# FFN input products: third unit's P5 and P4 ahead of the first P3, last unit's P7 ahead of P2, first weight sum on VectorE

## The chip, the cores and the metric

The kernel runs on one core of a Trainium2 chip. The metric is the device time of one execution in microseconds (us), lower is better. Three runs of the kernel before gave 786.75, 789.37 and 789.67 us (median 789.37). One further execution was profiled.

## The reference, cut to what matters

One layer of a hybrid decoder block on 512 tokens of width 1024, in float32: three parallel token mixers, a merge and an output projection, then a gated feed-forward network (FFN). The change is in the input product of the FFN:

```python
h2 = rms_norm(x, g_pre_ffn) * (1 + scale2) + shift2
gt, up = jnp.split(h2 @ w_ffn_in, 2, axis=-1)     # 1024 -> 2 x 2816
f = (jax.nn.silu(gt) * up) @ w_ffn_out            # 2816 -> 1024
x = x + (gate2 * rms_norm(f, g_post_ffn)).astype(x.dtype)
```

## The kernel before

**Three passes per product.** Every weight piece w is split into `hi` (a cast on ScalarE, line 155, to the fp32r type in which TensorE multiplies) and `lo = w - hi` (VectorE, lines 157 and 159). Activations are split alike (`hbh`, `hbl`; `tx`). A product takes three matmuls: hi x hi, hi x lo, lo x hi. TensorE therefore needs, for its first three matmuls, the cast, and for the third the subtraction as well.

**Seven products in place of eight.** The hidden width 2816 is cut into 11 units of 2 x 128 channels. Tokens are cut in two halves of 256. A unit's 2 x 2 block product is done by a Winograd scheme with seven products P1 to P7 (`step`, line 1203; each 24 matmuls of 256 columns: 2 halves of gate and up x 4 slices x 3 passes). P6 is added onto a copy of P1. P2 is accumulated onto P1's PSUM bank, **P3 onto P5's PSUM bank**. Before P3 may write that bank, VectorE has to have read P5 alone: `gated_m1` (lines 1244, 1245 and 1247) forms c2 from P7, P6 (in `u2`), P5 and P4, and its second instruction, line 1245, is the one that reads P5.

**Weights.** A unit has four weight blocks. P1, P2, P4 and P7 use one block each (P7 after `wsum3`, line 306, has added another to it). P5, P6 and P3 use a running sum `s`: `wsum` makes s, GpSimd then adds further blocks to it by accumulating DMAs (line 319) between these products. For the first unit, s is not made by VectorE: SyncE loads one block a second time straight into s (line 299), an accumulating DMA adds the other (line 301), and a further one does this unit's `wsum3` (line 302).

**What sets the order.** Around here the program is written out by hand, engine by engine (`manual_schedule`): each engine works off its instructions in the order in which the Python code issues them. The table `WINO` says in which order weight pieces are split. `step(u, q, o, start, stop, ahead)` first has pieces split up to `ahead` beyond the one that it uses, and then issues its 24 matmuls. There are four buffers for `hi` and four for `lo`, so a cast four pieces ahead waits until TensorE has done with the product that used the buffer before. Instructions that wait hold up all that stands behind them on the same engine. The first three units are interleaved with the making of the activations (lines 1335 to 1417; `tar`, `b22` and `t3r` are sums and differences of the four blocks of h2, `hbh[:, 2]` and `hbh[:, 3]` the operands of P3 and P5); units 3 to 10 run in a loop (from line 1419). DMAs are queued on SyncE (loads) and GpSimd (accumulating ones).

Of the kernel before, what the change touches and what calls it, by code (L numbers as in the profile page):

```python
# [32 lines left out]
def hybrid_block(ctx: ExitStack, tc, x, c, mod_w, mod_b, g_pre_mix, g_post_mix, g_pre_ffn,  # L33
# [120 lines left out]
    def split(hi, lo, src, defer=False):  # L154
        act.copy(hi, src)  # L155
        if defer:
            lows_.append(lambda: vec.tensor_tensor(lo, src, hi.bitcast(F32), ALU.subtract))  # L157
        else:
            vec.tensor_tensor(lo, src, hi.bitcast(F32), ALU.subtract)  # L159
# [92 lines left out]

    WINO = [(0, 1), (1, 1), (0, 2), (2, 1), (1, 2), (2, 2)]
    WINO += [(u, q) for q in (5, 7, 6, 4) for u in range(2)]
    WINO += [(0, 3), (2, 5), (1, 3), (2, 4), (3, 5), (2, 6), (3, 1), (2, 7), (3, 4), (2, 3)]
    WINO += [(3, q) for q in (6, 2, 7)]
    for u in range(4, NU):
        WINO += [(u, 5), (u - 1, 3)] + [(u, q) for q in (1, 4, 6, 2, 7)]
    WINO.append((NU - 1, 3))
    units = {u: {} for u in range(NU)}  # L260
    late_pool = {}
# [1 line left out]
    def wino_src(u, i, g):  # L263
        c0 = g * FFN + (2 * u + i) * P
        return w_ffn_in[:, c0:c0 + P].rearrange("(k p) n -> p k n", k=8)
# [19 lines left out]
        units[u][i] = [raw[:, :, 4 * a:4 * a + 4].rearrange("p g k n -> p g (k n)")  # L285
                       for a in range(2)]

    def wsum_tile():
        return late_pool["fx"].tile([P, 2, 512], F32, tag="wsum", name="wsum", bufs=2)

    def wsum(u):

        un = units[u]
        un["s"] = wsum_tile()
        if u:
            vec.tensor_tensor(un["s"], un[1][0], un[1][1], ALU.add)  # L296
            return
        for g in range(2):
            nc.sync.dma_start(un["s"][:, g].rearrange("p (k n) -> p k n", k=4),
                              wino_src(u, 1, g)[:, 0:4])  # L300
        nc.gpsimd.dma_start(un["s"], un[1][1], accum_op=ALU.add)
        nc.gpsimd.dma_start(un[1][0], un[0][0], accum_op=ALU.add)

    def wsum3(u):
        un = units[u]
# [829 lines left out]
    def chain_h2(tb):  # L1135
        for hf in range(2):
            vec.scalar_tensor_tensor(xms[tb][hf], xms[tb][hf], sts[tb][:, 5:6], SH[hf],
                                     op0=ALU.mult, op1=ALU.add)
# [112 lines left out]
    def third_of(u, p5, u2):  # L1251

        step(u, 3, p5, False, True)
        vec.tensor_tensor(u2, p5, u2, ALU.add)
        gated_m0(f4s[u], u2, 1)
# [20 lines left out]
    if True:  # L1276
        def begin(n):

            while at["split"] < wino0 + n:
                split_piece(True)  # L1280
        late_mm(2)
        chain_sq(2, pos[2])
        chain_norm(2, pos[2])
        late_mm(3)
        begin(2)
        chain_x1(2, pos[2], lambda: t2("sq2"))
        lows()
        chain_xm(2)
        chain_sq(3, pos[3])
        chain_norm2(2)  # L1290
        chain_norm(3, pos[3])
        ma.close()
        fp = ctx.enter_context(tc.tile_pool(name="fp", bufs=1, reuse_waits="tile"))
        fxs = ExitStack()
        fx = fxs.enter_context(tc.tile_pool(name="fx", bufs=1, reuse_waits="tile"))
        late_pool.update(fp=fp, fx=fx)
        pb_ = {1: [], 5: [], 6: [], 7: [], 4: []}

        def fresh(q, ahead=0):
            u = len(pb_[q])  # L1300
            pb_[q].append(bank(f"pf{q}"))
            step(u, q, pb_[q][-1], True, True, ahead)
        u2s = [temp("u2", 512, 2) for _ in range(2)] + [f4_tile("u2f")[:, 0, :]]

        def first(u):
            fresh(1)
            act.copy(u2s[u], pb_[1][u])

        def sixth(ahead=0):
            u = len(pb_[6])  # L1310
            fresh(6, ahead)
            vec.tensor_tensor(u2s[u], pb_[6][u], u2s[u], ALU.add)


        ta, b22, t3_ = (f4_tile(n) for n in ("tar", "b22", "t3r"))

        def k4(t_, u):
            return t_[:, u, :].rearrange("p (k t) -> p k t", k=4)

        def tx_tiles(q):  # L1320
            tx[q] = [[q2("tx", FR).rearrange("p (k t) -> p k t", k=2) for _ in range(2)]
                     for _ in range(2)]

        def parts_of(q, t_):
            t4 = t_.rearrange("p u (k t) -> p k u t", k=4)
            for k0 in (0, 2):
                split(*[t__[k0 // 2].rearrange("p k (u t) -> p k u t", u=2) for t__ in tx[q]],
                      t4[:, k0:k0 + 2], True)
        tks = [slice(u * P, (u + 1) * P) for u in range(2)]

        def t1_of(u):
            vec.tensor_tensor(k4(ta, u), raws2[0, u], pts[u][0], ALU.subtract)
            split(hbh[:, 3, :, tks[u]], hbl[:, 3, :, tks[u]], k4(ta, u), True)
            act.copy(k4(b22, u), pts[u][1])
            lows()
        for u in range(3):
            wino_load(u, 1)
            if u == 0:
                wsum(u)
        begin(3)  # L1340
        first(0)
        lows()
        begin(4)
        first(1)
        chain_x1(3, pos[3], lambda: temp("sg1", 512))
        chain_h2(2)
        step(0, 2, pb_[1][0], False, True, 0)
        pts[0] = h2_tr(2)
        lows()
        begin(5)  # L1350
        chain_norm2(3)
        chain_xm(3)
        lows()
        chain_h2(3)
        first(2)
        begin(6)
        t1_of(0)
        step(1, 2, pb_[1][1], False, True, 0)
        pts[1] = h2_tr(3)
        begin(7)  # L1360
        t1_of(1)
        step(2, 2, pb_[1][2], False, True, 0)
        wsum(1)
        begin(8)
        act.preload_act_table_set("silu_and_others")
        for u in range(2):
            vec.tensor_tensor(k4(t3_, u), k4(b22, u), pts[u][0], ALU.subtract)
        lows()
        fresh(5)
        tx_tiles(7)  # L1370
        parts_of(7, t3_)
        lows()
        begin(9)
        lows()
        f4s.append(f4_tile("f4"))
        gated_m0(f4s[0], pb_[1][0], 0)
        flush()
        wsum3(1)
        fresh(5)
        f4s.append(f4_tile("f4"))  # L1380
        gated_m0(f4s[1], pb_[1][1], 0)
        tx_tiles(6)
        begin(10)
        vec.scalar_tensor_tensor(ta, ta, -1.0, b22, op0=ALU.mult, op1=ALU.subtract)
        lows()
        parts_of(6, ta)
        lows()
        fresh(7)
        begin(11)
        lows()  # L1390
        f4s.append(f4_tile("f4"))
        fresh(7)
        gated_m0(f4s[2], pb_[1][2], 0)
        begin(12)
        for q in range(2):
            vec.tensor_tensor(k4(ta, q), raws2[1, q], k4(ta, q), ALU.add)
        lows()
        tx_tiles(4)
        sixth()
        parts_of(4, ta)  # L1400
        lows()
        begin(13)
        lows()
        for u in range(2):
            split(hbh[:, 2, :, tks[u]], hbl[:, 2, :, tks[u]], k4(b22, u))
        sixth(3)
        for u in range(2):
            fresh(4, 4)
            flush()
            gated_m1(f4s[u], pb_[4][u], pb_[5][u], pb_[7][u], u2s[u])  # L1410
        third_of(0, pb_[5][0], u2s[0])
        fresh(5, 4)
        third_of(1, pb_[5][1], u2s[1])
        fresh(4, 4)

        third = None
        for u in range(3, NU):
            f4s.append(f4_tile("f4"))
            last = u == NU - 1
            p5 = bank("pf5")  # L1420
            step(u, 5, p5, True, True)
            if u == 3:
                sixth(4)
            else:
                third()
            if last:
                t_ = fp.tile([P, 2, 2, T], FR, tag="raw4", name="fparts", bufs=1)
                f_parts(0, t_[:, 0], t_[:, 1])
            p1 = bank("pf1")
            step(u, 1, p1, True, True)  # L1430
            if u == 3:
                fresh(7, 4)
                gated_m1(f4s[2], pb_[4][2], pb_[5][2], pb_[7][2], u2s[2])
            p6 = bank("pf6")
            act.copy(p6, p1)
            p4 = bank("pf4")
            step(u, 4, p4, True, True)
            if u == 3:
                third_of(2, pb_[5][2], u2s[2])
            step(u, 6, p6, False, True)  # L1440
            u2 = temp("u2", 512, 2)
            act.copy(u2, p6)
            step(u, 2, p1, False, True)
            gated_m0(f4s[u], p1, 0)
            p7 = bank("pf7")
            step(u, 7, p7, True, True)
            gated_m1(f4s[u], p4, p5, p7, u2)
            third = lambda a_=(u, p5, u2): third_of(*a_)
        f_split(1)
        third()  # L1450
        flush()
# [98 lines left out]
```

## Time and profile before

| | |
|---|---|
| runs, us | 786.75, 789.37, 789.67 |
| profiled execution, us | 787.89 |
| its span (first to last instruction), us | 786.0 |
| TensorE busy | 751.2 us, 96% |
| VectorE busy | 543.4 us, 69% |
| ScalarE busy | 398.0 us, 51% |
| FFN input products | 423.96 to 655.45 us of the span |
| of these, TensorE waiting | 5.4 (line 1245) + 1.2 + 1.0 + 0.3 us |

The times are microseconds from the first instruction. PE is TensorE, DVE is VectorE, ACT is ScalarE, POOL is GpSimd, SP is SyncE. A row of the timeline gives the start, the duration, the engine, the line, the operation, output<-inputs and, in square brackets, how long the engine stood idle before it and what released it. Matmuls overlap: each of these lasts 0.28 us, while one starts every 0.118 us.

### The profile page before, as it was taken

The page shows a single profiled execution, that of the slowest core. Times are in us where ns is not written, and L with a number is a line of the kernel's source. Part 1 is how long each engine was busy: PE and PEld are TensorE (multiplying, and loading weights), DVE is VectorE, ACT ScalarE, POOL GpSimd, SP SyncE. Part 2 cuts the span into 40 slices and gives each one's busy share as a digit, 9 for nine tenths or more (in the row PEclk, how much of TensorE's full clock was granted, in tenths as well). Part 3 has the DMA queues.
Part 4 walks back from the last instruction along what each step waited for, and adds up shares of the span by engine and source line. Part 5 has one row for each costly group of instructions (what it writes and reads, how often), then busy time and mean ns, then how long its engine had stood idle before and what let it go on. Part 6 is the DMA issues. An engine that isn't in the chain of part 4 may idle for free. (4 is left out here: it accounts for less than half of the span.)

```text
span 786.0 us, 11271 instructions
## 1 busy us (share of the span) xinstructions
PE 751.2 (96%) x4357; PEld 649.7 (83%) x4357; DVE 543.4 (69%) x769; ACT 398.0 (51%) x648; POOL 147.5 (19%) x191
## 2 busy tenths in 40 slices
PE   3899999999999999999999989999999999999996
PEld 2679887777678888888888889999999997878885
DVE  5999968668848656455688898777777778653114
ACT  5566544665668356353477554444444454523112
POOL 4453422244521110202100211111111100000000
PEclk9999999999999999999999999999999999999998
DMA  9982341112424686865848977767667654553002
GB/s 282 296 245 91 108 156 59 54 54 67 149 88 147 216 209 226 232 222 120 285 146 224 182 146 158 179 146 160 154 148 162 153 143 164 203 185 110 28 1 107
DMA packets 121061, 121.94 MB, mean 155 GB/s; under 512 B 4076, under 2 KB 94240, under 8 KB 121008
## 3 DMA queue, kind: packets, MB, share of 16 engines
q1 hardware_dynamic: 110128, 100.15, 41.5%
q0 software_dynamic: 10112, 20.01, 13.6%
q10 hardware_dynamic: 768, 1.07, 0.4%
q8 instruction: 34, 0.56, 0.3%
q14 instruction: 19, 0.16, 0.1%
HBM read 102.86 MB, written 2.10 MB: 134 GB/s over the span
## 5 line engine op out<-in xcount | busy, mean ns | idle before, releaser
L155 ACT CAST whi<-wraw 128x1024 fp32r<-128x1024 f32 (+1 forms) x129 | 133.0, 1035 | 160.9 <-PE pgt L168 32.6
L159 DVE TENSOR_TENSOR wlo<-wraw,whi 128x1024 fp32r<-128x1024 f32 (+1 forms) x89 | 110.0, 1242 | 82.9 <-ACT whi L155 82.3
L1221 PE MATMUL pf<-hbh,whi 128*128 128x256 f32 x352 | 99.5, 283 | 5.7 <-DVE c L1245 5.4
L1221 PE MATMUL pf<-hbl,whi 128*128 128x256 f32 x352 | 99.1, 282 | 1.0 <-DVE hbl L157 1.0
L1221 PE MATMUL pf<-hbh,wlo 128*128 128x256 f32 x352 | 99.2, 282 | 0.3 <-DVE wlo L157 0.3
L1221 PE MATMUL pf<-tx,whi 128*128 128x256 f32 x528 | 94.9, 281 | 0.0
L1221 PEld LDWEIGHTS pf<-tx,whi 128*128 128x128 f32 x528 | 80.9, 188 | 0.0
L167 PE MATMUL pgt<-hh,whi 128*128 128x512 f32 x192 | 75.6, 394 | 0.0
L1221 PE MATMUL pf<-tx,wlo 128*128 128x256 f32 x264 | 74.5, 282 | 1.0 <-DVE wlo L157 0.9
L169 PE MATMUL pgt<-hh,wlo 128*128 128x512 f32 x192 | 75.2, 392 | 0.0
L168 PE MATMUL pgt<-hl,whi 128*128 128x512 f32 x192 | 75.0, 391 | 0.0
L1221 PEld LDWEIGHTS pf<-hbh,whi 128*128 128x128 f32 x352 | 66.9, 190 | 6.3 <-issue 3.9
L1221 PEld LDWEIGHTS pf<-hbl,whi 128*128 128x128 f32 x352 | 66.7, 189 | 1.2 <-DVE hbl L157 1.2
L1221 PEld LDWEIGHTS pf<-hbh,wlo 128*128 128x128 f32 x352 | 66.8, 190 | 0.5 <-DVE wlo L157 0.5
L169 PE MATMUL pfo<-whi,fparts 128*128 128x512 f32 x154 | 60.9, 395 | 0.0
L168 PE MATMUL pfo<-wlo,fparts 128*128 128x512 f32 x154 | 60.9, 395 | 0.0
L167 PE MATMUL pfo<-whi,fparts 128*128 128x512 f32 x154 | 60.8, 395 | 0.0
L319 POOL DMA_DIRECT2D wsum<-wraw x22 | 26.2, 1191 | 176.7 <-DVE wlo L157 176.7
L157 DVE TENSOR_TENSOR wlo<-wsum,whi 128x1024 fp32r<-128x1024 f32 x33 | 40.4, 1225 | 25.7 <-ACT whi L155 25.6
L157 DVE TENSOR_TENSOR wlo<-wraw,whi 128x1024 fp32r<-128x1024 f32 x40 | 48.8, 1221 | 12.8 <-ACT whi L155 12.8
L155 ACT CAST whi<-wsum 128x1024 fp32r<-128x1024 f32 x33 | 34.4, 1047 | 42.5 <-DVE wsum L296 18.7
L1221 PEld LDWEIGHTS pf<-tx,wlo 128*128 128x128 f32 x264 | 49.7, 188 | 1.6 <-DVE wlo L157 1.6
(394 smaller groups left out, 1687.1 us busy)
## 6 DMA issues: line engine op xcount, KB each, us to landing
wraw<-in_w_in_dram SPq DMA_DIRECT2D x20, 1024.0 KB, 5.2
wraw<-in_w_ffn_in_dram SPq DMA_DIRECT2D x40, 512.0 KB, 5.8
wraw<-in_mod_w_dram SPq DMA_DIRECT2D x16, 1024.0 KB, 6.2
wsum<-wraw POOLq DMA_DIRECT2D x23, 512.0 KB, 5.5
wraw<-in_w_ffn_out_dram SPq DMA_DIRECT2D x10, 1024.0 KB, 5.1
wraw<-in_mod_w_dram SPq DMA_DIRECT2D x16, 512.0 KB, 6.3
wraw<-in_w_o_dram SPq DMA_DIRECT2D x8, 1024.0 KB, 5.7
gate<-gate POOLq DMA_DIRECT2D x14, 256.0 KB, 4.0
```

The source lines that it names most:

```text
L155: act.copy(hi, src)
L157: lows_.append(lambda: vec.tensor_tensor(lo, src, hi.bitcast(F32), ALU.subtract))
L159: vec.tensor_tensor(lo, src, hi.bitcast(F32), ALU.subtract)
L167: pe.matmul(o, whi, xhi, start=start, stop=False)
L168: pe.matmul(o, whi, xlo, start=False, stop=False)
L169: pe.matmul(o, wlo, xhi, start=False, stop=stop)
L319: lows_.append(lambda: nc.gpsimd.dma_start(un["s"], un[0][q - 5], accum_op=ALU.add))
L1221: pe.matmul(o[:, cs], a_[:, g, k, :], b_, start=(start and g + k + part == 0), stop=(stop and k == 3 and part == 2), skip_group_check=True)
```

## The change

It has three parts. (1) The products of the third unit (u = 2): its P5 and P4 now come right after the P4 of units 0 and 1, ahead of the P3 of units 0 and 1. In `WINO` the pieces move likewise, and the order of (2, 6) and (3, 5) is exchanged, as are the steps P6 of unit 2 and P5 of unit 3. The two P4 steps of units 0 and 1 look 3 pieces ahead instead of 4. The splitting of `hbh[:, 2]`, the operand of P3, is issued after the first `gated_m1` instead of ahead of it. The sum s of unit 2 gets a buffer of its own in another pool. (2) In the last unit (u = 10) P7 is issued ahead of P2, so that P2 stands between P7 and P3. (3) The sum s of unit 0 is made by VectorE from the two weight blocks in SBUF, behind `chain_h2(3)`; the two loads into s and one accumulating DMA go, and the other accumulating DMA (this unit's `wsum3`) is issued behind the sum.

```diff
-    WINO += [(0, 3), (2, 5), (1, 3), (2, 4), (3, 5), (2, 6), (3, 1), (2, 7), (3, 4), (2, 3)]
+    WINO += [(2, 5), (2, 4), (0, 3), (1, 3), (2, 6), (3, 5), (3, 1), (2, 7), (3, 4), (2, 3)]
...
+        WINO += [(u, q) for q in ((2, 7) if u < NU - 1 else (7, 2))]
...
     def wsum(u):
         un = units[u]
-        un["s"] = wsum_tile()
-        if u:
-            vec.tensor_tensor(un["s"], un[1][0], un[1][1], ALU.add)
-            return
-        for g in range(2):
-            nc.sync.dma_start(un["s"][:, g].rearrange("p (k n) -> p k n", k=4),
-                              wino_src(u, 1, g)[:, 0:4])
-        nc.gpsimd.dma_start(un["s"], un[1][1], accum_op=ALU.add)
-        nc.gpsimd.dma_start(un[1][0], un[0][0], accum_op=ALU.add)
+        if u == 2:
+            un["s"] = late_pool["fp"].tile([P, 2, T], F32, tag="f4", name="wsum2", bufs=NU)
+        else:
+            un["s"] = late_pool["fx"].tile([P, 2, 512], F32, tag="wsum", name="wsum", bufs=2)
+        vec.tensor_tensor(un["s"], un[1][0], un[1][1], ALU.add)
...
         chain_h2(3)
+        wsum(0)
+        nc.gpsimd.dma_start(units[0][1][0], units[0][0][0], accum_op=ALU.add)
         first(2)
...
-        for u in range(2):
-            split(hbh[:, 2, :, tks[u]], hbl[:, 2, :, tks[u]], k4(b22, u))
+        for i in (1, 0):
+            wino_load(3, i)
         sixth(3)
         for u in range(2):
-            fresh(4, 4)
+            fresh(4, 3)
             flush()
             gated_m1(f4s[u], pb_[4][u], pb_[5][u], pb_[7][u], u2s[u])
+            if u == 0:
+                for tb in range(2):
+                    split(hbh[:, 2, :, tks[tb]], hbl[:, 2, :, tks[tb]], k4(b22, tb))
+        fresh(5, 4)
+        fresh(4, 4)
         third_of(0, pb_[5][0], u2s[0])
-        fresh(5, 4)
         third_of(1, pb_[5][1], u2s[1])
-        fresh(4, 4)
...
-            step(u, 2, p1, False, True)
-            gated_m0(f4s[u], p1, 0)
             p7 = bank("pf7")
-            step(u, 7, p7, True, True)
-            gated_m1(f4s[u], p4, p5, p7, u2)
+            for q in (7, 2) if last else (2, 7):
+                if q == 2:
+                    step(u, 2, p1, False, True)
+                    gated_m0(f4s[u], p1, 0)
+                else:
+                    step(u, 7, p7, True, True)
+                    gated_m1(f4s[u], p4, p5, p7, u2)
```

In the program before, this is TensorE's order at the end of unit 1's P4 (`pf4_4295`): P3 of unit 0 follows, which writes the bank `pf5_4033` of that unit's P5.

```order
L1221 MATMUL pf4_4295<-tx_4183,whi_4225 128x256
L1221 MATMUL pf4_4295<-tx_4181,wlo_4226 128x256
L1221 MATMUL pf5_4033<-hbh_3359,whi_4256 128x256
L1221 MATMUL pf5_4033<-hbl_3360,whi_4256 128x256
L1221 MATMUL pf5_4033<-hbh_3359,wlo_4257 128x256
```

In the changed program it is P5 of unit 2 that follows, in a bank of its own, `pf5_4331`; P4 of unit 2 comes next, and only then P3 of unit 0.

```order
L1215 MATMUL pf4_4295<-tx_4181,whi_4225 128x256
L1215 MATMUL pf4_4295<-tx_4179,wlo_4226 128x256
L1215 MATMUL pf5_4331<-hbh_3359,whi_4258 128x256
L1215 MATMUL pf5_4331<-hbl_3360,whi_4258 128x256
L1215 MATMUL pf5_4331<-hbh_3359,wlo_4259 128x256
```

VectorE at the same place before; `wlo_4257` belongs to P3 of unit 0, `wlo_4263` to P5 of unit 2, the three `c2_4291` are unit 0's `gated_m1`, the three `c2_4327` unit 1's.

```order
L157 TENSOR_TENSOR wlo_4217<-wraw_3784,whi_4216 128x1024
L159 TENSOR_TENSOR hbl_3360<-b22_3782,hbh_3359 128x4x128 x2
L157 TENSOR_TENSOR wlo_4226<-rawf_3795,whi_4225 128x1024
L1230 TENSOR_TENSOR f4_4146<-sg0_4185,pf1_3922 128x256
L1312 TENSOR_TENSOR u2_3779<-pf6_4224,u2_3779 128x512
L157 TENSOR_TENSOR wlo_4257<-wsum_3787,whi_4256 128x1024
L296 TENSOR_TENSOR wsum_4260<-rawf_3798,rawf_3801 128x1024
L157 TENSOR_TENSOR wlo_4263<-wsum_4260,whi_4262 128x1024
L1244 TENSOR_TENSOR c2_4291<-pf7_4114,u2_3778 128x512
L1245 SCALAR_TENSOR_TENSOR c2_4291<-pf5_4033,c2_4291 128x512
L1247 TENSOR_TENSOR c2_4291<-pf4_4255,c2_4291 128x512
L157 TENSOR_TENSOR wlo_4297<-wsum_4023,whi_4296 128x1024
```

VectorE there in the changed program; `wlo_4259` belongs to P5 of unit 2, `wlo_4297` to P4 of unit 2, and `wlo_4333` of P3 of unit 0 follows behind the second three c2 instructions.

```order
L157 TENSOR_TENSOR wlo_4215<-wraw_3784,whi_4214 128x1024
L157 TENSOR_TENSOR wlo_4226<-rawf_3790,whi_4225 128x1024
L296 TENSOR_TENSOR wsum2_4229<-rawf_3793,rawf_3796 128x1024
L1224 TENSOR_TENSOR f4_4144<-sg0_4183,pf1_3920 128x256
L1306 TENSOR_TENSOR u2_3779<-pf6_4224,u2_3779 128x512
L157 TENSOR_TENSOR wlo_4259<-wsum2_4229,whi_4258 128x1024
L1238 TENSOR_TENSOR c2_4287<-pf7_4112,u2_3778 128x512
L1239 SCALAR_TENSOR_TENSOR c2_4287<-pf5_4031,c2_4287 128x512
L1241 TENSOR_TENSOR c2_4287<-pf4_4257,c2_4287 128x512
L159 TENSOR_TENSOR hbl_3360<-b22_3782,hbh_3359 128x4x128 x2
L157 TENSOR_TENSOR wlo_4297<-rawf_3796,whi_4296 128x1024
L1224 TENSOR_TENSOR f4_4068<-sg1_4300,c2_4287 128x512
```

The subtraction for one further piece no longer stands ahead of unit 0's three c2 instructions, and the two `hbl` splits moved from ahead of them to behind them.

VectorE where unit 0's sum is made, in the changed program; the row with `wsum_3917` is new there, and all other rows stand in the order that they had before.

```order
L1131 SCALAR_TENSOR_TENSOR xm_3911<-xm_3911,st_3758,SHSC_2633 128x512
L296 TENSOR_TENSOR wsum_3917<-wraw_3784 128x1024
L1326 TENSOR_TENSOR tar_3781<-braw_3624,pt2_3893 128x512
L157 TENSOR_TENSOR wlo_3947<-wraw_3829,whi_3946 128x1024
L157 TENSOR_TENSOR hbl_3360<-tar_3781,hbh_3359 128x4x128
L1326 TENSOR_TENSOR tar_3781<-braw_3658,pt2_3978 128x512
L157 TENSOR_TENSOR wlo_3989<-wsum_3917,whi_3988 128x1024
L157 TENSOR_TENSOR hbl_3360<-tar_3781,hbh_3359 128x4x128
```

The sum sits between the last `xm` instruction and the first `tar` one, six rows ahead of the second `hbl` split on which P5 of unit 0 depends.

## Rows read from the trace of the kernel before

**Rows 1.** The page: span, and busy time of each engine
```profile
span 786.0 us, 11271 instructions
...
PE 751.2 (96%) x4357; PEld 649.7 (83%) x4357; DVE 543.4 (69%) x769; ACT 398.0 (51%) x648; POOL 147.5 (19%) x191
```
**Rows 2.** Waits of PE, 420 to 660: us in total, times, longest
```profile
PE pf L1221 <- DVE c L1245: 5.4, 2, 3.8
```
**Rows 3.** Timeline of PE around unit 0's P3
```profile
469.39 0.28 PE L1221 MATMUL pf<-tx,wlo 128*128 128x256 f32 x1
473.44 0.35 PE L1221 MATMUL pf<-hbh,whi 128*128 128x256 f32 x1 [3.77 <-DVE c L1245]
```
**Rows 4.** Windows: length, busy us (instructions) of each engine, PE clock, DMA
```profile
473.40:478.10 4.70, 4.66 (x27) 4.69 (x28) 4.53 (x7) 1.57 (x2) 0.06 (x1) 0.65 1.17 273
...
492.00:640.00 148.00, 148.00 (x1255) 148.00 (x1254) 111.17 (x123) 72.00 (x91) 17.87 (x15) 1.00 0.67 152
...
652.50:655.40 2.90, 2.85 (x24) 2.88 (x25) 2.90 (x5) 0.63 (x1) 0.00 (x0) 1.00 0.80 297
```
**Rows 5.** Timeline of DVE ahead of unit 0's P3
```profile
462.67 1.22 DVE L157 TENSOR_TENSOR wlo<-wraw,whi 128x1024 fp32r<-128x1024 f32 x1
463.80 1.29 DVE L159 TENSOR_TENSOR hbl<-b,hbh 128x512 fp32r<-128x512 f32 x2
465.01 1.22 DVE L157 TENSOR_TENSOR wlo<-rawf,whi 128x1024 fp32r<-128x1024 f32 x1
466.14 0.42 DVE L1230 TENSOR_TENSOR f<-sg,pf 128x256 f32<-128x256 f32 x1
466.47 0.69 DVE L1312 TENSOR_TENSOR u<-pf,u 128x512 f32<-128x512 f32 x1
...
468.33 1.23 DVE L296 TENSOR_TENSOR wsum<-rawf 128x1024 f32<-128x1024 f32 x1
470.74 1.23 DVE L157 TENSOR_TENSOR wlo<-wsum,whi 128x1024 fp32r<-128x1024 f32 x1 [1.19 <-ACT whi L155]
...
472.60 0.69 DVE L1245 SCALAR_TENSOR_TENSOR c<-pf,c 128x512 f32<-128x512 f32 x1
...
474.01 1.22 DVE L157 TENSOR_TENSOR wlo<-wsum,whi 128x1024 fp32r<-128x1024 f32 x1
```
**Rows 6.** Timeline of PE around the last unit's P3
```profile
650.67 0.28 PE L1221 MATMUL pf<-tx,wlo 128*128 128x256 f32 x1
652.55 0.35 PE L1221 MATMUL pf<-hbh,whi 128*128 128x256 f32 x1 [1.60 <-DVE c L1245]
```
**Rows 7.** Timeline of PE at the start of unit 0's P5
```profile
442.56 0.28 PE L1221 MATMUL pf<-hbh,wlo 128*128 128x256 f32 x1
443.14 0.39 PE L1221 MATMUL pf<-hbh,whi 128*128 128x256 f32 x1 [0.30 <-ACT hbh L155]
444.48 0.38 PE L1221 MATMUL pf<-hbl,whi 128*128 128x256 f32 x1 [0.96 <-DVE hbl L157]
```
**Rows 8.** Timeline of DVE around unit 0's sum
```profile
436.86 0.68 DVE L1332 TENSOR_TENSOR tar<-braw,pt 128x512 f32<-128x512 f32 x1
437.91 1.22 DVE L157 TENSOR_TENSOR wlo<-wraw,whi 128x1024 fp32r<-128x1024 f32 x1 [0.37 <-ACT whi L155]
...
442.60 1.23 DVE L157 TENSOR_TENSOR wlo<-wsum,whi 128x1024 fp32r<-128x1024 f32 x1 [2.26 <-ACT whi L155]
```
**Rows 9.** Timeline of ACT, 440 to 450
```profile
441.52 1.05 ACT L155 CAST whi<-wsum 128x1024 fp32r<-128x1024 f32 x1 [2.63 <-DMA wsum<-wraw]
...
449.00 1.04 ACT L155 CAST whi<-wraw 128x1024 fp32r<-128x1024 f32 x1
```
**Rows 10.** DMAs issued from 433 to 434: count, KB each, us to landing
```profile
wraw<-wraw POOLq DMA_DIRECT2D x1, 512.0 KB, 11.5
```
**Rows 11.** DMAs issued from 448 to 449
```profile
wsum<-wraw POOLq DMA_DIRECT2D x1, 512.0 KB, 5.2
```
**Rows 12.** Timeline of PE at unit 0's P4
```profile
463.51 0.40 PE L1221 MATMUL pf<-tx,whi 128*128 128x256 f32 x2
```

More of the change, by code (lines that the diff above doesn't have):

```diff
@@ L254, in hybrid_block @@
     WINO += [(u, q) for q in (5, 7, 6, 4) for u in range(2)]
-    WINO += [(0, 3), (2, 5), (1, 3), (2, 4), (3, 5), (2, 6), (3, 1), (2, 7), (3, 4), (2, 3)]
+    WINO += [(2, 5), (2, 4), (0, 3), (1, 3), (2, 6), (3, 5), (3, 1), (2, 7), (3, 4), (2, 3)]
     WINO += [(3, q) for q in (6, 2, 7)]
     for u in range(4, NU):
-        WINO += [(u, 5), (u - 1, 3)] + [(u, q) for q in (1, 4, 6, 2, 7)]
+        WINO += [(u, 5), (u - 1, 3)] + [(u, q) for q in (1, 4, 6)]
+        WINO += [(u, q) for q in ((2, 7) if u < NU - 1 else (7, 2))]
     WINO.append((NU - 1, 3))
@@ L286, in wino_load @@
                        for a in range(2)]
-    def wsum_tile():
-        return late_pool["fx"].tile([P, 2, 512], F32, tag="wsum", name="wsum", bufs=2)
     def wsum(u):
         un = units[u]
-        un["s"] = wsum_tile()
-        if u:
-            vec.tensor_tensor(un["s"], un[1][0], un[1][1], ALU.add)
-            return
-        for g in range(2):
-            nc.sync.dma_start(un["s"][:, g].rearrange("p (k n) -> p k n", k=4),
-                              wino_src(u, 1, g)[:, 0:4])
-        nc.gpsimd.dma_start(un["s"], un[1][1], accum_op=ALU.add)
-        nc.gpsimd.dma_start(un[1][0], un[0][0], accum_op=ALU.add)
+        if u == 2:
[3 more added lines that the diff above has]
+        vec.tensor_tensor(un["s"], un[1][0], un[1][1], ALU.add)
     def wsum3(u):
@@ L1337, in hybrid_block @@
             wino_load(u, 1)
-            if u == 0:
-                wsum(u)
         begin(3)
@@ L1419, in hybrid_block @@
             last = u == NU - 1
+            if u == 3:
+                sixth(4)
             p5 = bank("pf5")
             step(u, 5, p5, True, True)
-            if u == 3:
-                sixth(4)
-            else:
+            if u > 3:
                 third()
```

## Prediction

> **What bounds the kernel now.** I read the page first, for the share of each engine: TensorE is busy for 751.2 of 786.0 us, 96% [rows 1], so what can be gained without taking work away is TensorE's idle time and its time at a low clock. Second, TensorE's waits in the stretch of the FFN input products: the largest is for VectorE's line 1245, 5.4 us in two waits, the longer 3.8 [rows 2]. Third, TensorE's timeline at these two waits. At unit 0's P3 the last matmul of the P4 ahead starts at 469.39 and the first of P3 at 473.44 [rows 3]. At the last unit's P3 the two starts are 650.67 and 652.55 [rows 6]. Fourth, the windows. Undisturbed, 1255 matmuls take 148 us, or 0.118 us each; a product of 24 is 2.83 us. In the 4.70 us after the first wait, 3.77 us of idle TensorE, only 27 start, at a mean granted clock of 0.65, that is partly at the lower of its two levels, 1.2 in place of 2.4 GHz [rows 4]. From 492 on TensorE never waits until the last unit [rows 4]: what is gained before 492 is carried on to the end if nothing else comes late.
>
> Fifth, VectorE's own timeline, for what makes line 1245 late [rows 5]. Unit 0's three c2 instructions stand behind the subtraction at 470.74, which belongs to P5 of unit 2. It waited 1.19 us for its cast, and the cast had to wait for a buffer that unit 1's P4, the product just ahead of the wait, was still reading. So VectorE could not release P3 before TensorE had run dry.
>
> **Part 1, unit 2's P5 and P4 ahead of unit 0's P3.** What goes: the start is late by 473.44 - 469.39 - 0.12 = 3.93 us [rows 3], and 27 matmuls in 4.70 us in place of 27 x 0.118 = 3.19 is 1.51 us of low clock [rows 4]. Together 5.44 us.
>
> What may be late next has to be walked through on VectorE, with start-to-start times from rows 5 (subtraction 1.13, pair of hbl splits 1.21, sum 1.2, f 0.33, u 0.60; the subtraction at 470.74 and three c2 take 3.27 up to 474.01, so 2.1 for three c2). I put unit 0's P4 1.2 us earlier than before (from part 3), at 462.3 in place of 463.51 [rows 12], with its low part at 461.5 in place of 462.67. In the new order VectorE then has: P4's low part of unit 1 from 462.6, unit 2's sum 463.75, f 464.95, u 465.3. The low part of P5 of unit 2 needs its cast, 1.05 us long, behind the sum's end at 465.0: it starts at 466.2 and ends at 467.4. Unit 0's three c2 follow until 469.5, the hbl pair until 470.7, the low part of P4 of unit 2 until 471.95. Then f of unit 0 (as long as a c2) and unit 1's three c2, until 474.7, and the low part of unit 0's P3 until 475.95.
>
> TensorE meets that as follows. P4 of unit 0 starts at 462.3 and has its low part at 462.7, 0.15 later than wanted; with P4 of unit 1 it runs to 468.2. P5 of unit 2 is ready (467.4 against 468.45). P4 of unit 2 starts at 471.0; its third matmul wants the low part at 471.25 and gets it at 472.0: 0.7 us. P3 of unit 0 starts at 474.6, wants its low part at 474.85 and gets it at 475.95: 1.1 us. The c2 release itself (line 1245 by 468.8 for unit 0) is 6 us early. P3 of unit 1 starts at 478.6, with its low part at 477.1, and from there VectorE gains: in the steady stretch it has 111.17 us of work in 148 [rows 4], 2.1 us for each product of 2.83. So 1.8 us of new waits: part 1 is worth 5.44 - 1.8 = 3.6 us. The bounds: 5.44 if these low parts are not late, and about 2 if both slips are double. I take the walk, since each of its durations has a row.
>
> Behind the instruction that newly waits on ScalarE, the cast of P5 of unit 2 waiting for the sum, stand the two hbh casts of P3 and the cast of P4 of unit 2. They end at about 468.3 and are not wanted before 469.5 (hbl) and 471.0: hidden. The last slot on which P5 of unit 2 depends, the bank that f reads, is free at 465.3. The loads of unit 3 keep their place on SyncE's queue.
>
> **Part 2, last unit's P7 ahead of P2.** What goes: 652.55 - 650.67 - 0.12 = 1.76 us [rows 6]. P2 gives TensorE 2.83 us of work while VectorE needs some 1.6 us from P7's end to that of line 1245; nothing else is put ahead of these c2 on VectorE. The other way round, P7's weights need the block sum of `wsum3`, which now stands one product nearer; four pieces of look-ahead (4 x 2.83 us) cover that. Bounds 1.2 to 1.8 us; I take 1.76.
>
> **Part 3, unit 0's sum on VectorE.** Cost: one sum, 1.22 us as at 468.33 [rows 5], in a place where VectorE is the pace: it delays `tar` at 436.86 and what follows. Gain: VectorE stood idle for 2.26 us before the subtraction at 442.60, because the cast before it waited for the sum's DMA until 441.52 [rows 8, 9]. With the sum ready by 438.1, `tar`, low part and hbl split end 0.85 later (0.37 of idle before 437.91 is swallowed), and the low part of P5 starts at 441.2 in place of 442.60: VectorE is 1.4 us ahead, 1.2 after the next cast. TensorE at unit 0's P5 lost 443.14 - 442.56 - 0.12 = 0.46 and 444.48 - 443.14 - 0.12 = 1.22 us [rows 7]; the hbl split on which it depends now comes 1.4 us earlier, so some 1.3 goes. The next products go on waiting for VectorE's low parts by about as much as before, since VectorE moves by the same 1.2. I take 1.2; bounds 0 (VectorE absorbs nothing of the sum) and 1.7 (all of both slips).
>
> The DMAs: two loads of 256 KB leave SyncE's queue, so unit 1's and 2's loads behind them move up. One accumulating DMA leaves GpSimd's queue. The other is issued 5 us later, after the sum's end at 438.1 in place of 433.07, and P7 of unit 0 needs it: ScalarE's cast at 449.00 [rows 9], now at about 447.8. Before, it landed 11.5 us after issue, beside another DMA of its kind and the loads [rows 10]; alone, such a DMA took 5.2 [rows 11]. I take 5.2 (landing 443.4, 4 us early), since both neighbours are gone by then; with 11.5 it lands at 449.7, 1.9 late.
>
> **The sum.** 3.6 + 1.76 + 1.2 = 6.6 us, against the profiled execution's 787.89: 781.3. That execution lies 1.5 us below the median of the three runs shown, 789.37; against the median it is 782.8. I take 782.0, between the two.
>
> **Rivals.**
> (a) *No new waits.* VectorE has the low parts in time, because small slips before 462 give it more lead than I count. For it: VectorE has 1.2 us of idle at 470.74 that goes. Against it: in my walk it is busy without a break from 461.5 to 476. Gain 8.4, time about 780.2.
> (b) *The clock falls again.* The granted clock was 0.65 after the wait of 3.77 us [rows 3, 4] and stayed at 1.00 after the one of 1.60 [rows 4, 6]. My two new waits add up to 1.8 us within 4 us; should they act as one, 1.5 us of low clock comes back. Gain 5.1, time 783.5. The Trainium skill ("TensorE: Matmul & The Clock Gate", Part 1, "What's actually happening") says that the throttled clock is the default and that recent business alone lifts it; by that rule broken-up work can be as bad as one long wait, which the rows here leave open. By it the sum would be 6.6 - 1.5.
> (c) *The wait only moves.* The queue of VectorE holds TensorE up at P4 of unit 2 and at P3 of unit 0 for most of what is removed, 4 us in place of 1.8, say because the hbh casts come late. For it: both now stand behind a sum and a cast that waits for it. Gain 3 to 3.9 us: about 785.5, which counts as no change.
> (d) *Slower, by the late accumulating DMA.* It is issued 5 us later, and ScalarE's cast for unit 0's P7 waits for it, with all of ScalarE's and then VectorE's queue behind. Each microsecond past 447.8 is one for TensorE, plus 1.5 of clock if the wait is long. It would have to take 20 us from issue to landing to outweigh the 6.6; with 11.5, the longest in these rows, the gain is still 4.7. It decides against the change only from 458 or so on.
>
> **How the numbers follow.** My forecast (782.0; own range 780 to 784) 60%; (a) 14%; (b) 14%; (c) 8%; (d) 4%. The range from 778.5 to 785.9 takes in (a) from the lower run level, (b), and (c) at its better end. About 0.5%, or 4 us, is what a measurement of this kernel can tell from no change, given runs 2.9 us apart. Faster than that: the forecast, (a) and most of (b), 0.84. Within: (c) and a little of (b), 0.12. Slower 0.04.
>
> **What would show it.** TensorE's wait list in this stretch should have no more line 1245. A low-part wait (line 157) of 0.5 to 1 us should stand at P4 of unit 2 and at P3 of unit 0, and the clock should stay at 1.00 from 465 to 490. The wait for hbl at unit 0's P5 should shrink from 0.96 to below 0.4, and the last unit's P3 should follow P2 without a gap. From 492 on, TensorE should be some 5 us ahead of its place before. A wait of ScalarE for the accumulating DMA before unit 0's P7 cast would prove part 3 wrong, a wait of more than 2 us anywhere from 465 to 485 my walk.

## The result

| | before | after |
|---|---|---|
| median, us | 789.37 (7 runs, 786.75 to 789.67) | 783.56 (7 runs, 781.09 to 785.35) |
| profiled execution, us | 787.89 | 785.35 |
| start of the FFN input products in it, us | 423.96 | 427.71 |
| length of these products, us | 231.49 | 225.56 |

The ratio of the times is 0.9928, with a 95% interval of [0.991, 0.9945]: faster by 5.7 us, 4.3 to 7.1. 782.0 was predicted, with a range of 778.5 to 785.9.

The two profiled executions lie only 2.5 us apart, because the one of the changed kernel reached the changed stage 3.75 us later, although its instructions up to there are the same. Over all profiled executions of this document that start lies between 423.3 and 430.9 us. So executions are compared below by the length of the stage, from the first matmul of P1 to the first matmul of the output product: 5.93 us shorter.

The first view is the list of TensorE's waits from 420 to 660 us in the changed kernel (total, times, longest). It answers to [rows 2]; all matmuls of the products are line 1215 here.

```profile
PE pf L1215 <- DVE wlo L157: 2.4, 5, 0.9
PE pf L1215 <- ACT pf L1432: 1.1, 1, 1.1
```

The wait for c2, 5.4 us before, is gone. In its place stand waits for low parts (the `lo` of a weight piece), and one line that the prediction does not have: 1.1 us behind a copy of ScalarE. The timeline of TensorE has the two predicted waits:

```profile
475.17 0.38 PE L1215 MATMUL pf<-tx,wlo 128*128 128x256 f32 x1 [0.36 <-DVE wlo L157]
...
478.00 0.28 PE L1215 MATMUL pf<-hbl,whi 128*128 128x256 f32 x1
479.15 0.38 PE L1215 MATMUL pf<-hbh,wlo 128*128 128x256 f32 x1 [0.87 <-DVE wlo L157]
```

The first is P4 of unit 2, the second P3 of unit 0, which began at 477.88 without a wait; in [rows 3] it began 3.93 us late. By the distance of the starts less 0.118 they cost 0.52 and 1.03 us. Two windows of 5 us over them (length; busy us and instructions of PE, of its weight load PEld, of DVE, ACT and POOL; granted clock; DMA share and GB/s) show the full clock, where [rows 4] has 0.65:

```profile
472.00:477.00 5.00, 4.63 (x39) 4.43 (x39) 4.85 (x7) 2.52 (x3) 0.13 (x1) 1.00 1.19 262
479.00:484.00 5.00, 4.85 (x41) 4.85 (x42) 4.29 (x5) 1.67 (x2) 1.18 (x1) 1.00 0.49 133
```

At the last unit's P3, TensorE's starts run on at 0.12 us, against the 1.88 of [rows 6]:

```profile
650.33 0.28 PE L1215 MATMUL pf<-hbh,wlo 128*128 128x256 f32 x1
650.45 0.28 PE L1215 MATMUL pf<-hbh,whi 128*128 128x256 f32 x1
```

For part 3, VectorE's timeline has the sum, and the low part of unit 0's P5 without a wait in front (2.26 us in [rows 8]):

```profile
440.61 1.22 DVE L296 TENSOR_TENSOR wsum<-wraw 128x1024 f32<-128x1024 f32 x1
...
444.68 1.22 DVE L157 TENSOR_TENSOR wlo<-wsum,whi 128x1024 fp32r<-128x1024 f32 x1
```

The list of DMAs issued from 442 to 443 has the one accumulating DMA that is left here, with its time to landing (11.5 us in [rows 10]):

```profile
wraw<-wraw POOLq DMA_DIRECT2D x1, 512.0 KB, 5.0
```

The slips of 0.46 and 1.22 us at unit 0's P5 [rows 7] have gone altogether; the list above has no wait for hbh or hbl.

The new wait is at P6 of unit 9, in TensorE's timeline:

```profile
620.62 0.28 PE L1215 MATMUL pf<-tx,wlo 128*128 128x256 f32 x1
621.97 0.50 PE L1215 MATMUL pf<-tx,whi 128*128 128x256 f32 x2 [1.08 <-ACT pf L1432]
```

The chain of work that ended last shows how it came about, in order of time (start, us, what):

```profile
586.66 8.30 DMA wsum<-wraw
...
595.06 1.06 ACT whi L155
...
596.14 1.23 DVE wlo L157
597.37 1.14 DVE wraw L300
...
599.02 0.69 DVE u L1248
...
599.80 0.42 ACT sg L1223
600.22 0.48 ACT pf L1432
600.71 0.98 ACT whi L155
...
602.85 1.23 DVE wsum L296
...
604.18 1.06 ACT whi L155
...
605.26 1.24 DVE wlo L157
...
606.78 9.39 DMA wsum<-wraw
...
616.28 1.06 ACT whi L155
```

From 586.66 to 621.97 the chain does not pass through TensorE. Per unit it is a loop: the accumulating DMA behind P5, the cast and low part of P6, the addition for P7, two small instructions (u on VectorE, sg on ScalarE), the copy ahead of P6 (which stands behind sg on ScalarE), the next unit's sum, its cast and low part, and the next such DMA, 20.1 us later. TensorE's seven products take 19.84. Beside the loads the DMA takes 7.8 to 9.4 us in these units. So the weights lose on TensorE unit by unit, and what is left of their lead at unit 9 decides.

ScalarE's copies for units 4 and 9 show the pace of this loop, here before the change:

```profile
520.58 0.57 ACT L1435 COPY pf<-pf 128x512 f32<-128x512 f32 x1
...
621.13 0.58 ACT L1435 COPY pf<-pf 128x512 f32<-128x512 f32 x1
```

The same two copies in the changed kernel:

```profile
518.88 0.57 ACT L1432 COPY pf<-pf 128x512 f32<-128x512 f32 x1
...
621.34 0.58 ACT L1432 COPY pf<-pf 128x512 f32<-128x512 f32 x1
```

From unit 4 to unit 9 that is 20.11 us per unit before and 20.49 after. Counting TensorE's matmuls back from its late starts (19.84 us per unit), P6 of unit 4 was due 2.1 us after the copy's end in both kernels, and P6 of unit 9 was due 0.7 us after the copy's end before the change and 1.2 us ahead of it after. TensorE's earlier arrival had moved the loop along with it; what differs is the loop's pace.

**Account of the stage.** TensorE's late starts (the distance of two starts less 0.118 us, where that is over 0.15) add up to 4.64 us in the stage after, which leaves 220.92 us without waits. Before they add up to 9.23; with the same 220.92 that leaves 1.34 for the low clock, against 1.51 by the window in [rows 4].

| us | before | after |
|---|---|---|
| late starts at unit 0's P5 | 1.68 | 0 |
| four low-part waits, 448 to 466 | 1.86 | 1.86 |
| c2 at unit 0's P3 | 3.93 | 0 |
| low clock behind it | 1.3 | 0 |
| P4 of unit 2, P3 of unit 0 | 0 | 1.55 |
| P6 of unit 9 | 0 | 1.23 |
| last unit's P3 | 1.76 | 0 |

### The profile page after: what moved, and what is told of

Read it like the earlier page. It is cut to its first block, busy times and chain, and to the rows that moved or that the text cites. A ratio compares the mean times of both kernels' runs of the same rounds, so it can differ in the third digit from the quotient of the medians.

```text
span 783.4 us, 11262 instructions
## 1 busy us (share of the span) xinstructions
PE 753.9 (96%) x4357; PEld 651.6 (83%) x4357; DVE 542.9 (69%) x770; ACT 397.1 (51%) x648; POOL 145.7 (19%) x190
```

## Experiments

The three parts were run alone, beside the whole change. "Stage" is the length as above, in each run's profiled execution; differences of the medians are worked out from the ratio and its interval. Two profiles of the changed kernel differ by 0.7 us in the stage, so stages are compared together with the waits in them. Edits are cut to their main lines; `...` marks a cut.

**Part 1 alone.**

```diff
-    WINO += [(0, 3), (2, 5), (1, 3), (2, 4), (3, 5), (2, 6), ...
+    WINO += [(2, 5), (2, 4), (0, 3), (1, 3), (2, 6), (3, 5), ...
...
```


> The kernel before with part 1 alone (P5 and P4 of the third unit ahead of the first P3). Theory: 5.4 us go (3.93 of wait for c2 and 1.51 of low clock behind it), and low-part waits of some 0.5 at P4 of unit 2 and 1.0 at P3 of unit 0 come: 3.6 to 4.0 us faster than before, the granted clock at 1.00 in the 5 us behind unit 0's P3. Rival, the clock falls again: about 2 us faster, a clock below 0.9 there. Rival, part 1 is only good together with part 3 (without the 1.2 us that part 3 gives, VectorE is late and the new waits grow to 3 or more): 2.5 us faster or less. The last unit's wait of 1.6 us stays under all of them.

Measured: 786.22 us, ratio 0.9955 [0.9933, 0.9977], 3.6 us faster (1.8 to 5.3); stage 227.98, 3.51 shorter. The two waits are 0.86 and 1.03 us, and the 4.70 us behind the second have the full clock and 39 matmuls, where before had 27:

```profile
481.10:485.80 4.70, 4.62 (x39) 4.62 (x40) 4.10 (x5) 1.53 (x2) 1.20 (x1) 1.00 0.43 115
```

The theory holds; part 1 does not need part 3. No wait for a copy stands at unit 9, although TensorE reaches unit 3 some 3.6 us sooner after the stage's start than before; by the count of matmuls the copy at unit 9 is 0.2 us early.

**Part 2 alone.**

```diff
+        WINO += [(u, q) for q in ((2, 7) if u < NU - 1 else (7, 2))]
...
+            for q in (7, 2) if last else (2, 7):
...
```


> The kernel before with part 2 alone (last unit's P7 ahead of its P2). Theory: 1.76 us faster, no wait of TensorE between P2 and P3 of the last unit, and the first c2 wait of 3.8 us as before. Rival, the wait only moves, to P7's weights or behind P3: 0 to 0.5 us faster.

Measured: 787.6 us, ratio 0.9974 [0.995, 0.9999], 2.1 us faster (0.1 to 3.9); stage 229.95, 1.54 shorter. No wait stands at the last P3, and the one of 3.8 us stayed.

**Part 3 alone.**

```diff
-        if u:
-            vec.tensor_tensor(un["s"], un[1][0], un[1][1], ALU.add)
-            return
...
+        vec.tensor_tensor(un["s"], un[1][0], un[1][1], ALU.add)
...
+        wsum(0)
+        nc.gpsimd.dma_start(units[0][1][0], units[0][0][0], accum_op=ALU.add)
...
```


> The kernel before with part 3 alone (unit 0's sum on VectorE). Theory: 1.2 to 1.7 us off TensorE's time up to unit 0's P4 (the two slips at the start of its P5, 0.46 and 1.22, go), ScalarE waits for no accumulating DMA before unit 0's P7. At the end less may be left, since the wait for c2 before unit 0's P3 hangs on VectorE: if VectorE comes there 1.2 earlier too, 1.2 us faster in all. Rival, VectorE is not earlier at c2 (the sum's 1.2 us only fill its idle time) and the c2 wait grows by what TensorE gained: 0 us.

Measured: 788.37 us, ratio 0.9983 [0.9961, 1.0005]: within the interval no difference. TensorE's waits in its profile:

```profile
PE pf L1214 <- DVE c L1238: 5.4, 2, 3.8
PE pf L1214 <- ACT pf L1428: 1.5, 2, 1.1
```

The slips at unit 0's P5 (1.68) went and the c2 wait did not grow, as the theory has it. But waits for the copy came, at P6 of units 8 and 9, 0.58 and 1.28 us by their starts; the stage is 231.96, none the shorter. What part 3 gained at 443 was lost at 603 and 625. So these waits come with part 3, also where TensorE still has its long wait at unit 0's P3.

**The whole change again.**

> The changed kernel, unaltered, beside the three parts. Theory: 5.5 to 6.5 us faster than before, and the three parts alone add up to that within 1 us. Its profile in the first run showed one further wait of TensorE, 1.23 us at 621.97, at the end of a chain that begins with an accumulating DMA that landed 9.4 us after its issue. If that DMA is bound by the traffic of the loads that a TensorE further ahead has set off, the wait is here again, 0.8 to 1.5 us at the same product; if it was chance, it is absent here, and the stage from the first P1 to the first output product takes 224.3 us in place of 225.6.

Measured: 783.45 us, ratio 0.991 [0.9878, 0.9942], 7.1 us faster (4.6 to 9.6); by the ratios the parts alone add up to 6.9. Stage 226.27, 5.22 shorter than before; by the stage the parts add up to 4.6, against 5.9 and 5.2 for the whole. The wait at unit 9's P6 is there again, 1.61 us, so it is not chance. Parts 1 and 2 alone do not have it, part 3 alone has.

**VectorE's order at the new waits.** The splits of P3's operand move behind the low parts, and one more piece is split ahead ("low parts first"):

```diff
-            fresh(4, 3)
+            fresh(4, 3 + u)
             flush()
+            if u == 1:
+                lows()
+                for tb in range(2):
+                    split(hbh[:, 2, :, tks[tb]], hbl[:, 2, :, tks[tb]], k4(b22, tb))
             gated_m1(f4s[u], pb_[4][u], pb_[5][u], pb_[7][u], u2s[u])
-            if u == 0:
-                for tb in range(2):
-                    split(hbh[:, 2, :, tks[tb]], hbl[:, 2, :, tks[tb]], k4(b22, tb))
```


> The changed kernel with VectorE's order around unit 0's P3 altered: the low parts for P4 of unit 2 and P3 of unit 0 are made ahead of the hbl splits of P3 and ahead of unit 1's three c2 (c2 of unit 0 stays first). Theory: both new waits (0.52 and 1.03 us in the changed kernel) are VectorE's queue order and nothing else, so both go and TensorE is 1.5 us ahead from 480 on. Of that the end sees 1.5 less than the changed kernel only if the weight DMAs keep up; if the accumulating DMA at 606 is the limit, the wait at unit 9's P6 (1.2 to 1.6 us) grows to 2.7 to 3.1 and the end sees nothing. Rival: VectorE has too much work here, whatever its order; the waits move to P3 of unit 0 or 1 and stay at 1 us or more in total.

Measured: 781.33 us, ratio 0.9909 [0.9877, 0.9941]; stage 224.51, 1.1 and 1.8 shorter than in the two profiles of the changed kernel. Both waits went; new ones of 0.31 and 0.45 came at 487 and 499. So they were queue order, with the earlier split in it. That the wait at unit 9 would grow to 2.7 or more was wrong: TensorE was further ahead, and the wait is 1.04.

**The DMA of the loop replaced by VectorE** ("addition on VectorE").

```diff
-        if q in (5, 6):
+        if q == 5 and u > 3:
+            lows_.append(lambda: vec.tensor_tensor(un["s"], un["s"], un[0][0], ALU.add))
+        elif q in (5, 6):
```


> The changed kernel with the first of the two accumulating DMAs of units 4 to 10 (block 0's first half into the running sum, issued behind P5's low part) replaced by an addition on VectorE. Theory: the wait of 1.2 to 1.6 us at unit 9's P6 comes from this DMA's landing 9.4 us after issue beside the loads; without it no cast of ScalarE waits for a DMA there, the wait goes and the kernel is 1.2 to 1.6 us faster than the changed one. VectorE, 75% busy in the units 4 to 10, pays some 1.2 us per unit in its idle time. Rival: VectorE's extra 1.2 us per unit delay the low parts and c2, new waits of 0.3 us or more per unit come, 2 us slower than the changed kernel.

Measured: 781.66 us, ratio 0.9903 [0.9874, 0.9932]; stage 224.19, 1.4 and 2.1 shorter. The window from 500 to 640 of the changed kernel:

```profile
500.00:640.00 140.00, 138.92 (x1176) 138.71 (x1175) 103.88 (x115) 67.03 (x87) 16.50 (x14) 1.00 0.66 151
```

The same window of this kernel:

```profile
500.00:640.00 140.00, 140.00 (x1188) 140.00 (x1187) 113.67 (x126) 68.55 (x86) 9.02 (x8) 1.00 0.53 125
```

VectorE does 9.8 us more and TensorE does not wait once. ScalarE's copy ahead of P6 now comes every 19.84 us, at TensorE's pace, where it came every 20.5 us on average from unit 4 to unit 9 in the changed kernel. The DMA in the loop was the cause.

**Both edits**, run twice.

> Both edits, low parts first and the addition on VectorE. Theory (the weight path by DMA is what limits TensorE once it is further ahead): the gains add up, 2.7 to 3.1 us faster than the changed kernel, while the first edit alone gains less than 0.5. Rival (the wait at unit 9 is independent of how far ahead TensorE is): each edit alone gains its 1.2 to 1.6 and this one the sum as well.

> Both edits on the changed kernel, unaltered, again. Theory: 223.6 us for the stage as before (220.8 with no wait at all and 2.8 of waits), no wait at unit 9's P6, 2.0 to 2.5 us faster than the changed kernel at the end. Rival: its lack of that wait was chance, 225 us or more.

Measured: 781.1 us, ratio 0.991 [0.9879, 0.994], and 780.48, 0.9892 [0.9871, 0.9914]; stages 223.58 and 223.46. The waits left, from the second:

```profile
PE pf L1217 <- DVE wlo L157: 1.4, 4, 0.6
PE pf L1217 <- DVE c L1241: 0.3, 1, 0.3
```

By the stage it is 2.0 to 2.8 us faster than the changed kernel, and the fastest version here. The intervals at the end overlap with those of the changed kernel; the stage tells them apart. The first edit alone had already shortened the stage by 1.1 to 1.8, so the statement that it would gain under 0.5 without the other was wrong: the wait at unit 9 is not set by how far ahead TensorE is, as the rival has it. The sum of the two gains alone, 2.5 to 3.9, is reached at its lower end at best.

**A long wait put back.** Four repeated operations, without effect on the values, delay the low part of unit 0's P3:

```diff
+        if again:
+            vec.tensor_tensor(c2[:, 0, :], p7, u2, ALU.add)
+            vec.tensor_tensor(c2[:, 0, :], p7, u2, ALU.add)
+            vec.scalar_tensor_tensor(c2[:, 1, :], p5, -1.0, c2[:, 0, :], op0=ALU.mult,
+                                     op1=ALU.subtract)
+            vec.tensor_tensor(c2[:, 0, :], p4, c2[:, 0, :], ALU.subtract)
...
```


> The changed kernel with four repeated c2 operations of 0.72 us each on VectorE ahead of the low part of unit 0's P3, so that TensorE's wait there grows from 1.03 to about 3.9 us, as long as the wait that the change took away. Theory: a wait of that length costs the clock too, as it did before: the granted clock falls below 0.8 in the 5 us behind it, 1.5 us more; TensorE is 4.4 us later at unit 3 than in the changed kernel. Rival: the low clock of before was bound to another cause at that place, the clock stays at 1.00 and TensorE is only 2.9 us later. The end may see up to 1.5 us less of it, since the wait at unit 9 has then no cause.

Measured: 787.54 us, ratio 0.9981 [0.9964, 0.9997]; stage 231.63, 6.1 and 5.4 longer than in the changed kernel. TensorE's timeline at the wait:

```profile
474.86 0.28 PE L1215 MATMUL pf<-hbl,whi 128*128 128x256 f32 x1
478.90 0.58 PE L1215 MATMUL pf<-hbh,wlo 128*128 128x256 f32 x1 [3.76 <-DVE wlo L157]
```

The windows behind it, columns as above:

```profile
478.85:483.55 4.70, 4.65 (x22) 4.65 (x23) 4.70 (x5) 1.56 (x2) 1.18 (x1) 0.50 0.10 19
483.55:485.55 2.00, 2.00 (x13) 2.00 (x13) 2.00 (x3) 1.05 (x1) 0.13 (x1) 0.68 1.09 188
485.55:488.00 2.45, 2.45 (x23) 2.45 (x22) 2.00 (x3) 1.20 (x2) 1.05 (x1) 1.00 0.55 87
```

The wait is as long as the one removed (3.76 against 3.77 us), and the clock fell to the lower level, 1.2 GHz. 22 matmuls in 4.70 us in place of 39.8, and 13 in 2.00 in place of 16.9, are 2.6 us. With a wait of 1.03 us at this place the changed kernel kept the full clock, so the low clock is a cost of the long wait and not of the place. Its size was forecast too small: 1.5 us before, 2.6 here. In parts 2 and 3 alone, where the old wait of 3.77 us stayed, 27 and 26 matmuls start in the 4.70 us behind it, at 0.64: 1.5 and 1.6 us. Why the same length cost more here is open. The end of the forecast was wrong too: with TensorE some 5.6 us later at unit 3, P6 of units 7 and 9 waits for the copy all the same, 0.46 and 1.15 us by the starts.

**Two loads put back.** Their data is not used.

```diff
+            if u == 0:
+                s_ = units[0]["s"] = fx.tile([P, 2, 512], F32, tag="wsum", name="wsum", bufs=2)
+                for g in range(2):
+                    nc.sync.dma_start(s_[:, g].rearrange("p (k n) -> p k n", k=4),
+                                      wino_src(0, 1, g)[:, 0:4])
...
```


> The changed kernel with the two loads of 256 KB that part 3 took away put back (into the buffer of unit 0's sum, which VectorE overwrites later; their data is not used). From the copy ahead of unit 4's P6 on, the loop of weight transfers took 125.2 to 126.0 us to unit 9's copy in the kernels without part 3 and 126.3 to 127.9 in those with it. Theory: the loop is slower by the place at which the loads stand in their queue; with the two loads back it takes 126 or less and the wait at unit 9's P6 (1.2 to 1.6 us) is below 0.5. Rival: part 3 slows it by its timing alone (or the difference is chance): 127 to 128 us, the wait stays above 1.

Measured: 782.24 us, ratio 0.9915 [0.9897, 0.9933]; stage 224.53, 1.0 and 1.7 shorter than in the changed kernel. (The interval named there begins at unit 3's copy, not unit 4's.) The loop took 125.7 us, and the wait at unit 9 is gone:

```profile
PE pf L1217 <- DVE wlo L157: 2.8, 5, 0.9
```

The six accumulating DMAs behind P5 of units 4 to 9 took 50.1 us in all from issue to landing, against 51.6 in the changed kernel. So the absence of these loads lengthened transfers that come some 75 to 180 us later. The other profiles agree: from unit 4's copy to unit 9's the loop took 20.11 to 20.27 us per unit in the four kernels with the two loads (before, parts 1 and 2 alone, this one), and 20.32 to 20.64 in the five profiles without them that have the loop's DMA. By which way (the place in the queue, or when the loads behind them fall) this run cannot tell; it stays open.

**Both edits without part 3.**

```diff
-        wsum(0)
-        nc.gpsimd.dma_start(units[0][1][0], units[0][0][0], accum_op=ALU.add)
...
```


> Parts 1 and 2 with both edits (low parts first, addition on VectorE), but unit 0's sum by DMA as in the kernel before. Theory: part 3 is worth the two slips at unit 0's P5 (0.3 to 0.5 and 1.2) and little else: the stage of the input products takes 225.0 to 225.5 us, against 223.6 with part 3. Rival: part 3 gives VectorE no lasting lead and other waits shrink as these come back: 224.2 or less.

Measured: 781.76 us, ratio 0.9908 [0.9889, 0.9926]; stage 224.27, 0.7 to 0.8 longer than with part 3. One slip of 0.64 at unit 0's P5 came back, not 1.5 to 1.7. The stage lies close to the rival's: part 3 is worth 0.7 to 0.8 us once the loop is no limit.

**Sums on GpSimd.**

```diff
-        vec.tensor_tensor(un["s"], un[1][0], un[1][1], ALU.add)
+        (vec if u > 1 else nc.gpsimd).tensor_tensor(un["s"], un[1][0], un[1][1], ALU.add)
...
```


> Both edits, and the sums of units 0 and 1 on GpSimd, ahead of its DMAs, where it stands idle from 385 to 442 us; GpSimd took 1.42 to 1.71 us for 128x512, so an estimated 3.4 us for each. Theory: VectorE is the pace from 440 to 466 and has 2.4 us less to do; TensorE's four small waits there (0.43, 0.46, 0.78, 0.19) shrink to 0.6 or less in sum, 1.2 us faster than with both edits alone. Rival: while GpSimd adds, VectorE is slowed by as much (its operations of 1.22 us take 2 us or more beside it) or the sums come later than the casts want them: 0 to 1 us slower.

Measured: 782.24 us, ratio 0.9915 [0.9894, 0.9937]; stage 223.98, 0.4 to 0.5 longer than both edits alone. The small waits from 448 to 466 did shrink, to 0.19, but one of 1.51 us came at 442.72. The second sum in GpSimd's timeline:

```profile
436.90 3.41 POOL L298 TENSOR_TENSOR wsum<-rawf 128x1024 f32<-128x1024 f32 x1 [1.20 <-DMA rawf<-in_w_ffn_in_dram]
```

VectorE's timeline, with the same 128x1 operation undisturbed and beside that sum:

```profile
429.00 0.15 DVE L1130 TENSOR_TENSOR st<-st 128x1 f32<-128x1 f32 x1
...
437.98 2.35 DVE L1130 TENSOR_TENSOR st<-st 128x1 f32<-128x1 f32 x1
440.25 1.28 DVE L1126 TENSOR_TENSOR xm<-x,SHSC 128x512 f32<-128x512 f32 x2
```

TensorE's late start behind it:

```profile
442.72 0.39 PE L1219 MATMUL pf<-hbh,wlo 128*128 128x256 f32 x1 [1.51 <-DVE wlo L157]
```

The tiny VectorE operation ended when GpSimd's sum did, at 440.3. The rival holds.

## Why the prediction was right, and where not

- **Part 1.** 5.44 us to be removed: confirmed as 3.93 of wait and 1.3 to 1.5 of low clock, and that the clock belongs to the wait is shown by the long wait put back. The walk on VectorE forecast new waits of 0.7 and 1.1; 0.52 and 1.03 came. Part 1 is worth 3.6 by forecast, 3.7 in the account and 3.5 to 3.6 alone. Rival (c), the wait only moves, is out: 1.55 in place of 4. Rival (a), no new waits, is out too, though another order on VectorE makes it nearly true.
- **Rival (b), the clock.** The waits of 0.36 and 0.87 us within 4 us left it at 1.00; 3.76 in one piece brought it to 0.50. The Trainium skill ("TensorE: Matmul & The Clock Gate", Part 1, "What's actually happening") says that the throttled clock is the default and that activity releases the throttle. The rows agree for the long wait; work broken up by two short ones kept the clock.
- **Part 2.** 1.76 forecast, 1.76 in the profile, 1.5 and 2.1 alone.
- **Part 3.** 1.2 forecast; both slips at unit 0's P5 went whole, 1.68, the upper bound. The DMA of rival (d) landed 5.0 us after issue, close to the 5.2 taken. But part 3 alone made the kernel no faster: with the wait at unit 9 that comes with it, 1.23, some 0.45 is left in the whole change. The gain came where it was forecast, and most of it was lost at unit 9.
- **The step that failed** is in the reading of what bounds the kernel: "From 492 on TensorE never waits until the last unit [rows 4]: what is gained before 492 is carried on to the end if nothing else comes late." Something did. The row is right, but it shows no slack. Before the change, ScalarE's copy for unit 9's P6 ended 0.7 us ahead of TensorE; the DMA loop was already the slower of the two, 20.1 us per unit on average against 19.84. Part 3 made it slower still, 20.5 and 20.6 in the two profiles, and 1.2 to 1.6 us were given back there. Of the two loads that go, the prediction says only that the loads behind them move up; what that does to the loop it put at nothing. That TensorE came earlier is not what decided. At unit 3, counted from the stage's start, the changed kernel is 5.5 us ahead of the kernel before; part 1 alone is 3.6 ahead and the kernel with the two loads back 5.1, and neither waits at unit 9. Part 3 alone is 1.6 ahead and the kernel with the long wait put back not at all, and both wait.
- **Luck in the total.** Without this wait the stage would have gained 7.2 us; the sum said 6.6 and the stage gave 5.9. The misses have opposite signs, so the total looks better than its terms.
- **A reading that was wrong.** The prediction has the cast of unit 2's P5 wait for a buffer that unit 1's P4 was reading. The profile does put that wait down to TensorE:

```profile
469.67 1.99 ACT L155 CAST whi<-wsum 128x1024 fp32r<-128x1024 f32 x2 [5.52 <-PE pf L1221]
```

But with four buffers, the one it takes is that of the piece four places before in `WINO`, unit 1's P6, and P4 of unit 0 had followed that product at 463.51 [rows 12]. The cast starts 0.11 us after unit 2's sum ends on VectorE (468.33 + 1.23 us [rows 5]). In the changed kernel the same cast starts 0.11 us after the sum as well (467.02 + 1.22), and there the profile names it:

```profile
468.35 1.05 ACT L155 CAST whi<-wsum 128x1024 fp32r<-128x1024 f32 x1 [4.10 <-DVE wsum L296]
```

So VectorE's own queue held the cast, and with it c2. The forecast does not rest on the buffer: its walk has the cast wait for the sum.

## What to carry to other kernels

An engine that never waits over many units shows nothing of its margin: find the loops that feed it (who issues the transfer, what waits for it, what starts the next one), take their length per unit, and compare it with the engine's. A chain of waits that stays off the busiest engine for nearly two units, as here from 586.66 to 621.97, is a sign of such a loop. That the busiest engine gets ahead need not bring such a wait, if the loop starts at that engine's own pace: here the margin at unit 4 was 2.1 us with and without the gain, and a slower loop used it up. A wait of nearly 4 us on TensorE is priced with the low clock behind it, here 40 to 70% on top.

## What the hardware did unexpectedly

- Waits of the same length cost 1.5 to 1.6 us of low clock in three kernels (3.77 us) and 2.6 in a fourth (3.76 us).
- An accumulating DMA of 512 KB within SBUF took 5.0 us alone; behind P5 of units 4 to 9, beside the loads, it took 7.0 to 9.7.
- GpSimd's 128x1024 sum held up VectorE even in a 128x1 operation, 2.35 us in place of 0.15. The Trainium skill ("SBUF — State Buffer", "Who interferes with whom") says that a VectorE instruction with two SBUF inputs contends with a GpSimd instruction that reads SBUF, and that issue order, not the shape of the operation, decides who blocks. The trace agrees: this operation has two SBUF inputs, it came 1.08 us after the sum had started, and it ended with the sum.
- Two loads of 256 KB more or fewer changed how long other transfers took over 75 us later: 50.1 in place of 51.6 us for six of them.
